# A Mamba/GLA trunk: decay broadcasts on ScalarE's queue, weight stores on SyncE's, block sums in three stages, PSUM banks shared out anew

## The chip, the cores and the metric

One core of one Trainium2 chip runs the whole kernel. The metric is the device time of one launch in microseconds (us). Before the change three runs gave 2479.24, 2486.99 and 2486.57 us, a median of 2486.57 us.

## What is computed

The reference is one layer of a hybrid decoder over 2048 tokens and 16 meta tokens, width 1024. One input projection feeds two branches, their results are gated and merged, and an output projection follows.

```python
u = rmsnorm(hres, norm_w)
proj = jnp.einsum('bld,dn->bln', u, w_in)
z, xbc, dt_raw, q, k, v, g_gla, a_lr, merge_g = split_cols(proj, IN_WIDTHS)
xbc = jax.nn.silu(causal_depthwise_conv(xbc, conv_w, conv_b))
dt = jax.nn.softplus((dt_raw + dt_bias).astype(jnp.float32))
y_r, _ = ssd_chunked(xs[:, m:], dt[:, m:], a, bm[:, m:], cm[:, m:], SSD_CHUNK, s_m)
y_ssd = rmsnorm((y.reshape(b, l, D_SSD) * jax.nn.silu(z)).reshape(...), ...)   # 4 groups of 4 heads
o_r, _ = gla_chunked(q[:, m:], k[:, m:], v[:, m:], log_a[:, m:], GLA_CHUNK, st_m)   # 4 heads
y_gla = o.reshape(b, l, GLA_DV) * jax.nn.silu(g_gla)
branch_proj = jnp.einsum('blnc,ncd->blnd', branches, w_branch)
merged = jnp.sum(gates * branch_proj, axis=2)
return hres + jnp.einsum('bld,de->ble', merged, w_out)      # then a final rmsnorm
```

Within an SSD chunk the scores are multiplied by `exp(da_cum[t] - da_cum[s])`, so each chunk needs the cumulative decay of its four heads broadcast to all 128 partitions.

## The kernel before

**Two phases.** The first runs to 1667 us of the profile. It takes the tokens in four blocks of 512 and does the projections and the scans of both branches. The second does the gate, branch and output matmuls by a scheme of seven products in place of eight, for which sums of quarter blocks (`sums`) are needed as moving operands.

**The first phase, per block.** Four SSD groups (`ssd_proj`, `ssd_scan`) and then four GLA heads (`gla_proj`, `gla_scan`). The projection generators run in the foreground. At each of their `yield`s the main loop calls `step()`, which advances every background generator by one step: the scan of the group before, the `gates`, the load of the next block's `u`, and a unit of block sums (`beside_unit`). A group or head has 6 steps. TensorE (PE) and SyncE (SP) execute in exactly this written order (`manual_schedule`); the orders of ScalarE (ACT), VectorE (DVE) and GpSimd (POOL) come from a scheduler.

**Matmuls.** Each product in high precision is three matmuls (`accum`, L174 to L176: high by high, high by low, low by high). `proj_feat` makes 128 features by all tokens of the block: 24 matmuls of 512 columns per half weight, or, in block 0, where the 16 meta tokens come first, two segments of 264 columns in two PSUM banks. `proj_tok` makes tokens by 256 features for z (SSD) and v (GLA): four chunks of 128 tokens, each in a PSUM bank of its own, although it fills half of one.

**Weights.** In block 0 `load_w` loads each weight tile to `wr` (3 buffers, L160), ACT copies the high part to `whl` (4 buffers, L161), POOL subtracts to get the low part (L162), and the pair is stored to DRAM from ACT's queue (`save`, L170). There are 100 such tiles. Blocks 1 to 3 load the kept pair in one DMA (L157, names `k_s`, `k_z`, `k_g`, `k_v`, `k_zm`). A load waits until PE has done with the tile four before it.

**Decay broadcasts.** `dt_chain` transposes the cumulative decay, ACT copies it to `th` (L385) and stores it to the DRAM tile `cumd` (L386). `fetch_cb` loads one chunk's rows back, broadcast over partitions, to `cb` (2 buffers, L468, 64 DMAs on SP). The first of a group is issued after that group's third feature projection, the next ones in `before(c)` of the scan. ACT reads `cb` in the Relu at L527.

**Block sums.** `make_sums` loads four 128x256 pieces to two `wr` tiles on SP (L76), subtracts on POOL (L80) in the same step, and stores four results from ACT's queue (L84) one step later. Six units of eight such pieces run in the first phase, one (`late`) in the second.

**PSUM.** Eight banks: four `pj` (projections and gates), two `pt` (transposes), two `pc` (scan matmuls). At the end of an SSD scan two transposes into `pt` are read by ACT (L575); at the end of a GLA scan two are read by DVE (L779). The next transposes on PE are those of another scan: L483 and L515 (SSD), L686 and L691 (GLA). Feature projections are read from `pj` by ACT at L447 and L448 (SSD) and L588 (k of GLA), and the gates at L411.

Of the kernel before, what the change touches and what calls it, by code (L numbers as in the profile page):

```python
# [14 lines left out]
P = 128  # L15
# [25 lines left out]
def trunk_kernel(ctx: ExitStack, tc: tile.TileContext, xm, xmt, w_feat, w_tok, w_zm, w_br, w_o,  # L41
# [24 lines left out]

    HB = BLK // 2
# [3 lines left out]
    def make_sums(pool, tag, nb, braw, sums, j, c, store):  # L71
        cs = slice(c * HB, (c + 1) * HB)
        room = [mk(pool, [P, 512], F32, tag, bufs=nb) for _ in range(2)]
        room = [t[:, i * HB:(i + 1) * HB] for t in room for i in range(2)]
        for r, (k, t) in zip(room, ((0, 1), (0, 0), (1, 1), (1, 0))):
            nc.sync.dma_start(r, braw(4 * k + j, t)[:, cs])  # L76
        b12, b11, b22, b21 = room
        todo = []
        for i, (o, x, y) in enumerate(((b11, b12, b11), (b12, b22, b12), (b22, b22, b11), (b21, b21, b22))):
            nc.gpsimd.tensor_tensor(o, x, y, op=ALU.subtract)  # L80
            todo.append((sums[(0, 2, 1, 3)[i]][j][:, cs], o))
        yield
        for dst, src in todo:
            store.dma_start(dst, src)  # L84

    def new_sums(name):
        return [[left(f"{name}_t{i}_{j}") for j in range(4)] for i in range(4)]
# [31 lines left out]
    pj = first.enter_context(tc.tile_pool(name="pj", bufs=4, space=bass.MemoryType.PSUM))  # L119
    pt = first.enter_context(tc.tile_pool(name="pt", bufs=2, space=bass.MemoryType.PSUM))  # L120
# [32 lines left out]
    def load_w(key, src):  # L153
# [4 lines left out]
        else:  # L158
            raw = mk(wpool, [P, 512], F32, "wr", bufs=NWR)[:, :n]
# [7 lines left out]
    def save(n):  # L167

        while len(unsaved) > n:
            nc.scalar.dma_start(*unsaved.pop(0))  # L170
# [19 lines left out]
    def proj_tok(key, src, u, starts, pools, width=256, per=2, sub=None):  # L190


        pss = [bank(*pl) for pl in pools]
        nq = KT // per
        for q0 in range(0, nq, 2):
# [3 lines left out]
            for i, (ps, a) in enumerate(zip(pss, starts)):  # L199
                c0 = sub if sub is not None and i >= NCH else 0  # L200
                for k2 in range(2 * per):
# [4 lines left out]
                          (h[:, cs], lo[:, cs]), kt == 0, kt == KT - 1)  # L206
        return pss
# [131 lines left out]
    def dt_chain(o, psd):  # L339
# [44 lines left out]
        cr = mk(wk, [P, META + BLK], F32, "th", bufs=1)[:NH, :BLK]  # L384
# [39 lines left out]
    def ssd_proj(o, g):  # L424
# [3 lines left out]
        if g == 0:  # L428
            pools = [(pj, "pj")] * NCH + ([(pc, "pc")] if m0 else [])
            pss = yield from proj_tok("zm", w_zm, o.u, o.starts + [0] * o.ci0, pools, 288, 1, 256)  # L430
            begin(dt_chain(o, pss[NCH:] + pss[:NCH]))
            pss = pss[:NCH]
        else:
            pss = yield from proj_tok(f"z{g}", w_tok[g], o.u, o.starts, [(pj, "pj")] * NCH)
        for c, ps in enumerate(pss):
            zt = mk(wk, [P, 256], F32, "zt", bufs=1)
            nc.scalar.activation(zt, ps[:, :256], AF.Tanh, scale=0.5)
            nc.vector.scalar_tensor_tensor(zs[:, c], zt, 1.0, ps[:, :256], op0=ALU.add, op1=ALU.mult)
        yield
        for j in range(4):  # L440
# [13 lines left out]
            th = mk(wk, [P, META + BLK], F32, "th", bufs=1)[:, :tt]  # L454
            nc.scalar.activation(th, acc, AF.Tanh)
            f = mk(wk, [P, META + BLK], F32, "act", bufs=NACT)
            nc.vector.scalar_tensor_tensor(f[:, :tt], th, 1.0, acc, op0=ALU.add, op1=ALU.mult)
            feats.append(f)
            if j == 2:
                fetch_cb(o, g, 0)  # L460
# [5 lines left out]
    def fetch_cb(o, g, c):  # L466
        cbs[g, c] = cb = mk(wk, [P, 4, P], F32, "cb")
# [654 lines left out]
```

## Time and profile before

| | |
|---|---|
| median of three runs | 2486.57 us |
| the profiled execution, its own time | 2480.0 us |
| its span, first to last instruction | 2478.2 us |
| first phase, blocks 0, 1, 2, 3 (from the start) | 0 to 455, to 848, to 1242, to 1667 us |
| second phase | 1667 to 2478 us |
| PE busy | 2295.6 us (93%) |
| DVE, ACT, POOL busy | 1584.5, 1192.5, 736.9 us |
| mean granted clock of TensorE | 0.964 |

A row of waits reads "who, at which line and tile, waited for whom: us in total, times, longest us". A row of a timeline reads "start us, us, engine, line, operation, tiles, count" and in brackets the idle time just before, with what ended it. Rows that begin with SPq or ACTq are of an engine's queue, which issues DMAs and waits in order. Rows of windows give the stretch, its length, the busy time of PE, weight loads, DVE, ACT and POOL, the granted clock, the share of the DMA engines, and GB/s. A matmul's own duration overlaps the next one's: what matters is the distance of starts.

### The profile page before, as it was taken

How to read it: one execution, taken by the hardware profiler on the slowest of the kernel's cores; microseconds unless marked ns; L12 is line 12 of the kernel's file. 1: busy time of each engine (PE TensorE's matmuls, PEld its weight loads, DVE VectorE, ACT ScalarE, POOL GpSimd, SP SyncE). 2: the span in 40 equal slices, each digit the busy share in tenths (PEclk: the TensorE clock that was granted, in tenths of full speed). 3: DMA queues.
4: the chain of work that ended last, by engine and by line, in shares of the span. 5: the costliest groups of instructions: out<-in, count | busy, mean ns of one | idle time of the engine just before them, and what ended most of it. 6: DMA issues, size and time to landing. Idle time of an engine off the chain costs nothing. (4 is left out here: it accounts for less than half of the span.)

```text
span 2478.2 us, 37092 instructions
## 1 busy us (share of the span) xinstructions
PE 2295.6 (93%) x12641; PEld 1989.2 (80%) x12641; DVE 1584.5 (64%) x2913; ACT 1192.5 (48%) x2820; POOL 736.9 (30%) x713
## 2 busy tenths in 40 slices
PE   6899999979989989999989999979999999999898
PEld 6789889868878977888877888858888778888676
DVE  3577665656566557655546565576478874788865
ACT  4565555445543346444335543445455444553443
POOL 2334433122320122231022112245433642335431
PEclk8899999989999999999999999979999999999999
DMA  7555765466785556686465567657477853777653
GB/s 252 201 181 212 269 242 188 158 218 216 232 273 179 178 173 223 222 264 207 156 203 190 180 196 233 203 171 258 146 263 247 270 197 108 259 236 261 211 158 127
DMA packets 303342, 518.10 MB, mean 209 GB/s; under 512 B 29488, under 2 KB 145456, under 8 KB 303152
## 3 DMA queue, kind: packets, MB, share of 16 engines
q1 hardware_dynamic: 246128, 414.65, 52.3%
q10 hardware_dynamic: 57024, 101.08, 10.9%
q8 instruction: 99, 1.62, 0.3%
q14 instruction: 91, 0.75, 0.1%
HBM read 368.42 MB, written 147.19 MB: 208 GB/s over the span
## 5 line engine op out<-in xcount | busy, mean ns | idle before, releaser
L174 PE MATMUL pj<-u,whl 128*128 128x512 f32 (+1 forms) x1184 | 454.1, 384 | 50.4 <-DMA whl<-k_s 31.7
L176 PE MATMUL pj<-u,whl 128*128 128x512 f32 (+1 forms) x1184 | 437.5, 370 | 1.5 <-POOL whl L162 1.5
L175 PE MATMUL pj<-u,whl 128*128 128x512 f32 (+1 forms) x1184 | 437.0, 369 | 0.0
L174 PE MATMUL pj<-whl,u 128*128 128x256 f32 (+1 forms) x1024 | 303.8, 297 | 14.7 <-ACT u L273 6.5
L174 PEld LDWEIGHTS pj<-u,whl 128*128 128x128 f32 x1184 | 231.0, 195 | 92.4 <-DMA whl<-k_s 35.3
L175 PE MATMUL pj<-whl,u 128*128 128x256 f32 (+1 forms) x1024 | 297.3, 290 | 1.6 <-POOL whl L162 1.5
L176 PE MATMUL pj<-whl,u 128*128 128x256 f32 (+1 forms) x1024 | 296.9, 290 | 1.4 <-DVE u L275 1.4
L176 PEld LDWEIGHTS pj<-u,whl 128*128 128x128 f32 x1184 | 229.5, 194 | 38.8 <-POOL whl L162 2.1
L175 PEld LDWEIGHTS pj<-u,whl 128*128 128x128 f32 x1184 | 230.8, 195 | 34.1
L174 PE MATMUL psa<-b,a 128*128 128x512 f32 x640 | 249.0, 393 | 3.4 <-ACT b L870 1.9
L175 PE MATMUL psa<-b,a 128*128 128x512 f32 x640 | 250.6, 392 | 0.1
L176 PE MATMUL psa<-b,a 128*128 128x512 f32 x640 | 247.3, 391 | 0.4 <-DVE a L892 0.4
L174 PEld LDWEIGHTS pj<-whl,u 128*128 128x128 f32 x1024 | 201.3, 197 | 17.2 <-DMA whl<-k_v 7.1
L452 DVE SCALAR_TENSOR_TENSOR acc<-cin,hcw,acc 128x512 f32<-128x512 f32 (+1 forms) x192 | 154.3, 803 | 80.3 <-ACT acc L448 79.5
L175 PEld LDWEIGHTS pj<-whl,u 128*128 128x128 f32 x1024 | 201.2, 196 | 3.0 <-POOL whl L162 2.7
L176 PEld LDWEIGHTS pj<-whl,u 128*128 128x128 f32 x1024 | 201.1, 196 | 1.9 <-DVE u L275 1.8
L162 POOL TENSOR_TENSOR whl<-wr,whl 128x512 fp32r<-128x512 f32 (+1 forms) x100 | 132.4, 1333 | 200.6 <-ACT whl L161 131.8
L871 DVE TENSOR_TENSOR b<-br,b 128x512 fp32r<-128x512 f32 x196 | 168.0, 898 | 25.1 <-ACT b L870 25.1
L80 POOL TENSOR_TENSOR wr<-wr 128x256 f32<-128x256 f32 x96 | 74.8, 779 | 318.2 <-DMA wr<-y 161.7
L882 POOL TENSOR_TENSOR as<-ar,ar 128x512 f32<-128x512 f32 x40 | 59.8, 1496 | 328.5 <-DMA ar<-in_w_br 106.0
L892 DVE TENSOR_TENSOR a<-ar,a 128x512 fp32r<-128x512 f32 x160 | 140.6, 891 | 20.7 <-ACT a L891 20.6
L174 PEld LDWEIGHTS psa<-b,a 128*128 128x128 f32 x640 | 121.3, 190 | 30.4 <-ACT sn L908 2.7
(259 smaller groups left out, 5100.5 us busy)
## 6 DMA issues: line engine op xcount, KB each, us to landing
whl<-k_s SPq DMA_DIRECT2D x96, 512.0 KB, 5.3
whl<-k_g SPq DMA_DIRECT2D x96, 512.0 KB, 4.2
whl<-k_v SPq DMA_DIRECT2D x48, 512.0 KB, 4.2
whl<-k_z SPq DMA_DIRECT2D x36, 512.0 KB, 4.1
wr<-in_w_feat SPq DMA_DIRECT2D x64, 256.0 KB, 4.4
k_s<-whl ACTq DMA_DIRECT2D x32, 512.0 KB, 4.3
cb<-cumd SPq DMA_DIRECT2D x64, 256.0 KB, 5.2
y<-gg ACTq DMA_DIRECT2D x64, 256.0 KB, 3.0
```

Source lines behind the costliest of these rows:

```text
L80: nc.gpsimd.tensor_tensor(o, x, y, op=ALU.subtract)
L162: nc.gpsimd.tensor_tensor(hl[:, 1], raw, hl[:, 0].bitcast(F32), op=ALU.subtract)
L174: nc.tensor.matmul(ps, sh, mh, start=first, stop=False, **kw)
L175: nc.tensor.matmul(ps, sh, ml, start=False, stop=False, **kw)
L176: nc.tensor.matmul(ps, sl, mh, start=False, stop=last, **kw)
L452: nc.vector.scalar_tensor_tensor(acc, cin[:, k:k + tt], hcw[:, ti, k:k + 1], acc, op0=ALU.mult, op1=ALU.add)
L871: nc.vector.tensor_tensor(t[:, 1], raw, t[:, 0].bitcast(F32), op=ALU.subtract)
L882: nc.gpsimd.tensor_tensor(s1, a21, a22, op=ALU.add)
L892: nc.vector.tensor_tensor(t[:, 1], src, t[:, 0].bitcast(F32), op=ALU.subtract)
```

## The change

1. `fetch_cb` issues on ACT's queue, `cb` has 3 buffers, and the first fetch of a group moves from the projection to the start of its scan.
2. The kept weights of block 0 are stored from SP: `load_w` calls `save(2)` just ahead of each new load.
3. `make_sums` has a step for the loads, one for the subtractions and one for the stores; two results that lie side by side are stored in one DMA. A unit takes 24 steps where it took 16. The units are placed at group 0 and group 4, five in the first phase, two in the second.
4. Two chunks of z (groups 1 to 3) and of v share a bank; they are read in operations of 512 columns. `pj` has 3 banks, `pt` has 3. The fourth chunk of the first z lies in a `pt` bank.
5. The tiles `th` and `zt` are gone: tanh is written to its destination and multiplied in place. The copy for `cumd` uses a `cin` buffer.

```diff
     def make_sums(pool, tag, nb, braw, sums, j, c, store):
         cs = slice(c * HB, (c + 1) * HB)
-        room = [mk(pool, [P, 512], F32, tag, bufs=nb) for _ in range(2)]
-        room = [t[:, i * HB:(i + 1) * HB] for t in room for i in range(2)]
-        for r, (k, t) in zip(room, ((0, 1), (0, 0), (1, 1), (1, 0))):
+        pair = [mk(pool, [P, 512], F32, tag, bufs=nb).rearrange("p (i c) -> p i c", i=2) for _ in range(2)]
+        for r, (k, t) in zip((t[:, i] for t in pair for i in range(2)), ((0, 1), (0, 0), (1, 1), (1, 0))):
             nc.sync.dma_start(r, braw(4 * k + j, t)[:, cs])
...
+        yield
+        (b12, b11), (b22, b21) = [(t[:, 0], t[:, 1]) for t in pair]
+        for o, x, y in ((b11, b12, b11), (b12, b22, b12), (b22, b22, b11), (b21, b21, b22)):
             nc.gpsimd.tensor_tensor(o, x, y, op=ALU.subtract)
         yield
-        for dst, src in todo:
-            store.dma_start(dst, src)
+        for dst, src in zip(sums, pair):
+            store.dma_start(dst[j][:, :, cs], src)
...
-    beside = {(1, 0): ("o",)}
+    beside = {(1, 0): ("o",), (1, 4): ("g", 0)}
+    late = []
     for s in range(nsb):
-        b = 2 * s + 1
-        if b + 1 < nblk:
-            beside.update({(b, 3): ("g", s), (b + 1, 0): ("b", 0, s), (b + 1, 3): ("b", 1, s)})
+        b = 2 * s + 2
+        if b < nblk:
+            beside.update({(b, 0): ("b", 0, s), (b, 4): ("b", 1, s)})
         else:
-            beside.update({(b, 0): ("g", s), (b, 5): ("b", 0, s)})
-    late = [("b", 1, nsb - 1)]
+            late += [("b", 0, s), ("b", 1, s)]
+        if 0 < s:
+            beside[b - 1, 0] = ("g", s)
...
-    pj = first.enter_context(tc.tile_pool(name="pj", bufs=4, space=bass.MemoryType.PSUM))
-    pt = first.enter_context(tc.tile_pool(name="pt", bufs=2, space=bass.MemoryType.PSUM))
+    pj = first.enter_context(tc.tile_pool(name="pj", bufs=3, space=bass.MemoryType.PSUM))
+    pt = first.enter_context(tc.tile_pool(name="pt", bufs=3, space=bass.MemoryType.PSUM))
...
         else:
+            save(2)
             raw = mk(wpool, [P, 512], F32, "wr", bufs=NWR)[:, :n]
             nc.sync.dma_start(raw, src)
...
         while len(unsaved) > n:
-            nc.scalar.dma_start(*unsaved.pop(0))
+            nc.sync.dma_start(*unsaved.pop(0))
...
                     accum(ps[:, c0:width], tuple(t[:, kt, a:a + P] for t in u),
-                          (h[:, cs], lo[:, cs]), kt == 0, kt == KT - 1)
-        return pss
+                          (h[:, cs], lo[:, cs]), bk not in opened, kt == KT - 1, skip_group_check=True)
+                    opened.add(bk)
+
+    def halves_of(pool, tag):
+
+        bks = [bank(pool, tag) for _ in range(2)]
+        return bks, [(i // 2, bks[i // 2][:, i % 2 * 256:(i % 2 + 1) * 256]) for i in range(4)]
...
-        cr = mk(wk, [P, META + BLK], F32, "th", bufs=1)[:NH, :BLK]
+        cr = mk(wk, [P, 3 + META + BLK], F32, "cin")[:NH, :BLK]
...
-        for c, ps in enumerate(pss):
-            zt = mk(wk, [P, 256], F32, "zt", bufs=1)
-            nc.scalar.activation(zt, ps[:, :256], AF.Tanh, scale=0.5)
-            nc.vector.scalar_tensor_tensor(zs[:, c], zt, 1.0, ps[:, :256], op0=ALU.add, op1=ALU.mult)
+            pss, places = halves_of(pj, "pj")
+            yield from proj_tok(f"z{g}", w_tok[g], o.u, o.starts, places)
+            done = [(ps, zs[:, 2 * r:2 * r + 2].rearrange("p c f -> p (c f)")) for r, ps in enumerate(pss)]
+        for ps, dst in done:
+            nc.scalar.activation(dst, ps, AF.Tanh, scale=0.5)
+            nc.vector.scalar_tensor_tensor(dst, dst, 1.0, ps, op0=ALU.add, op1=ALU.mult)
...
             feats.append(f)
-            if j == 2:
-                fetch_cb(o, g, 0)
             yield
...
-        cbs[g, c] = cb = mk(wk, [P, 4, P], F32, "cb")
-        nc.sync.dma_start(cb, o.cumd[4 * g:4 * g + 4, c * P:(c + 1) * P].unsqueeze(0).to_broadcast([P, 4, P]))
+        cbs[g, c] = cb = mk(wk, [P, 4, P], F32, "cb", bufs=3)
+        nc.scalar.dma_start(cb, o.cumd[4 * g:4 * g + 4, c * P:(c + 1) * P].unsqueeze(0).to_broadcast([P, 4, P]))
 
     def ssd_scan(o, g, feats, zs):
...
         x0, x1, bf, cf = feats
+        fetch_cb(o, g, 0)
         yield
```

On SP the decay fetch leaves the stream of weight loads. Before, block 1, from the second feature of group 0 to the first z weight of group 1 (`whl` weight tiles, `cb` a decay broadcast, `wr` pieces of the block sums):

```order
L157 DMA whl_5689<-k_s_0_757 128x1024
L157 DMA whl_5703<-k_s_1_787 128x1024
L157 DMA whl_5789<-k_s_0_844 128x1024
L157 DMA whl_5803<-k_s_1_874 128x1024
L468 DMA cb_5830<-cumd_5318 128x4x128
L76 DMA wr_5852<-in_w_o 128x256 x2
L76 DMA wr_5853<-in_w_o 128x256 x2
L157 DMA whl_5863<-k_s_0_925 128x1024
L157 DMA whl_5877<-k_s_1_955 128x1024
L157 DMA whl_5918<-k_z_0_1007 128x1024
```

After, the same place:

```order
L159 DMA whl_5534<-k_s_0_696 128x1024
L159 DMA whl_5548<-k_s_1_727 128x1024
L76 DMA wr_5620<-in_w_o 128x256 x2
L76 DMA wr_5621<-in_w_o 128x256 x2
L159 DMA whl_5635<-k_s_0_782 128x1024
L159 DMA whl_5649<-k_s_1_813 128x1024
L159 DMA whl_5700<-k_s_0_860 128x1024
L159 DMA whl_5714<-k_s_1_891 128x1024
L159 DMA whl_5750<-k_z_0_939 128x1024
```

The weights of the fourth feature (`k_s_0_925`, now `k_s_0_860`) and of z no longer stand behind `cb`, and the pieces of the block sums stand one projection earlier here.

On ACT, block 0, group 0, the fetches now stand right behind the store of `cumd`. Before (`pj` are projection banks, `th` the copy that is stored):

```order
L385 ACTIVATE th_832<-pt_827 16x512
L447 ACTIVATE cin_899<-pj_837 128x264
L448 ACTIVATE acc_900<-pj_837,hcb,hcw 128x264
L447 ACTIVATE cin_899<-pj_838 128x264
L448 ACTIVATE acc_900<-pj_838,hcb,hcw 128x264
L386 DMA cumd_442<-th_832 16x512
L161 ACTIVATE whl_920<-wr_921 128x512
```

After:

```order
L394 ACTIVATE cin_771<-pt_766 16x512
L395 DMA cumd_386<-cin_771 16x512
L164 ACTIVATE whl_933<-wr_935 128x512
L455 ACTIVATE cin_838<-tails 128x3
L475 DMA cb_995<-cumd_386 128x4x128
L465 ACTIVATE act_763<-acc_753 128x528
L455 ACTIVATE cin_916<-tails 128x3
L475 DMA cb_1094<-cumd_386 128x4x128
L475 DMA cb_1214<-cumd_386 128x4x128
L457 ACTIVATE cin_838<-pj_774 128x264
L458 ACTIVATE acc_839<-pj_774,hcb,hcw 128x264
```

Three fetches are issued together, ahead of the third feature's evacuation. The order on PE is the same in both kernels.

More of the change, by code (lines that the diff above doesn't have):

```diff
@@ L188, in proj_feat, with proj_tok @@
         return pss
-    def proj_tok(key, src, u, starts, pools, width=256, per=2, sub=None):
-        pss = [bank(*pl) for pl in pools]
+    def proj_tok(key, src, u, starts, banks, width=256, per=2, sub=None):
         nq = KT // per
+        opened = set()
         for q0 in range(0, nq, 2):
@@ L592, in gla_proj @@
         vm = None
+        pss, places = halves_of(pj, "pj")
         if m0:
             vm = mk(wk, [P, 256], F32, "c1", bufs=NC1)[:META]
[L595 to L601 removed]
+            pv5 = bank(pt, "pt")
+            places.append((2, pv5[:, :256]))
+        yield from proj_tok(f"v{h}", w_tok[SG + h], o.u, o.starts + [0] * o.ci0, places)
+        if m0:
+            nc.scalar.activation(vm, pv5[:META, :256], AF.Copy)
+        for r, ps in enumerate(pss):
+            split(*[t[:, 2 * r:2 * r + 2].rearrange("p c f -> p (c f)") for t in (vh, vl)], ps)
         yield
@@ L814, in trunk_kernel @@
                     step()
-                    save(2)
             save(0)
@@ L1027, in trunk_kernel @@
                 gen = make_sums(rpl, "tb", 2, *sums[key], j, c, nc.sync)
-                for _ in range(2):
-                    at(i, lambda gen=gen: next(gen, None))
-                    i += 3
+                for k in range(3):
+                    at(i + 2 * k, lambda gen=gen: next(gen, None))
+                i += 5
     for fn in todo.get(-1, []):
```

37 lines of the change are left out of this document (12 added, 25 removed).

## The prediction

> **What bounds the kernel now.** I read the page first, then the waits of PE, then of SP, then timelines around the longest waits, and the granted clock in windows last.
>
> ```profile
> span 2478.2 us, 37092 instructions
> PE 2295.6 (93%) x12641; PEld 1989.2 (80%) x12641; DVE 1584.5 (64%) x2913; ACT 1192.5 (48%) x2820; POOL 736.9 (30%) x713
> ```
>
> PE is the bound, and the other engines have room on average. The change takes no matmul away and leaves PE's order as it was, so all it can win is PE's idle time, 2478.2 - 2295.6 = 183 us, and time in which PE runs at a lower clock. The next view names what PE waited for.
>
> ```profile
> PE pj L174 <- DMA whl<-k_s: 31.7, 8, 8.7
> PE pt L515 <- DVE gg L779: 14.0, 3, 5.3
> PE pj L174 <- ACT whl L161: 12.6, 3, 7.3
> PE pt L691 <- ACT gg L575: 12.1, 4, 5.4
> PE pj L174 <- DMA whl<-k_v: 5.3, 4, 2.1
> PE pt L483 <- ACT gg L575: 5.0, 3, 2.5
> PE pj L174 <- DMA whl<-k_g: 4.5, 2, 2.3
> PE pt L686 <- ACT gg L575: 1.9, 1, 1.9
> ```
>
> There are two families. One waits for weights, though in blocks 1 to 3 these come ready from DRAM. The other (L483, L515, L686, L691) are transposes that wait for a `pt` bank until the last two transposes of the scan before are read. The long waits of the first family, in order of time:
>
> ```profile
> 74.92 0.59 PE L174 MATMUL pj<-u,whl 128*128 128x264 f32 x1 [7.34 <-ACT whl L161]
> 503.68 0.80 PE L174 MATMUL pj<-u,whl 128*128 128x512 f32 x1 [8.68 <-DMA whl<-k_s]
> 896.96 0.80 PE L174 MATMUL pj<-u,whl 128*128 128x512 f32 x1 [7.95 <-DMA whl<-k_s]
> 1289.96 0.79 PE L174 MATMUL pj<-u,whl 128*128 128x512 f32 x1 [8.13 <-DMA whl<-k_s]
> ```
>
> One per block, at the same place: the fourth feature of group 0. SP's own waits, then its timeline, then one row of ACT's say why.
>
> ```profile
> SPq L160 <- POOL whl L162: 215.6, 74, 9.1
> SPq L468 <- ACT sq L527: 138.8, 23, 18.9
> SPq L468 <- DMA cumd<-th: 73.8, 4, 20.8
> ...
> 471.04 3.04 SPq L157 DMA_DIRECT2D whl<-k_s  x2
> 494.91 0.37 SPq L468 DMA_DIRECT2D cb<-cumd  x1
> 495.38 1.88 SPq L76 DMA_DIRECT2D wr<-in_w_o  x4
> 497.35 0.86 SPq L157 DMA_DIRECT2D whl<-k_s  x2
> ...
> 493.32 0.32 ACTq L386 DMA_DIRECT2D cumd<-th  x1
> ```
>
> SP issued weights until 474.08, then stood for 20.8 us in front of the decay fetch, because ACT stored `cumd` only at 493.32; it had landed when the fetch went out at 494.91. The weights behind it in SP's order were issued at 497.35, and PE stood until 503.68. The four such waits (73.8 us on SP) answer to the four on PE.
>
> **The clock.** After such a wait PE also runs slower for a while.
>
> ```profile
> 503.70:508.70 5.00, 5.00 (x12) 3.94 (x13) 0.00 (x0) 0.00 (x0) 0.00 (x0) 0.50 0.89 320
> 549.60:553.00 3.40, 3.39 (x14) 3.21 (x15) 3.40 (x8) 0.24 (x2) 0.00 (x0) 0.52 0.27 101
> 943.70:949.00 5.30, 5.29 (x18) 4.74 (x19) 5.30 (x13) 0.69 (x3) 0.65 (x1) 0.50 0.28 103
> 1336.90:1341.60 4.70, 4.68 (x17) 4.22 (x18) 4.70 (x12) 0.41 (x2) 0.65 (x1) 0.50 0.30 112
> 745.00:835.00 90.00, 89.22 (x553) 79.98 (x553) 52.16 (x129) 38.30 (x107) 4.39 (x2) 1.00 0.53 169
> ```
>
> Behind the 8.68 us wait the granted clock is 0.50 for 5 us, so 2.5 us more are lost. Behind the three waits at L515 (549.61, 943.7, 1336.9) it is 0.50 to 0.52 for 3.4, 5.3 and 4.7 us, a loss of 1.6 + 2.65 + 2.35 = 6.6 us. The last row is the counterexample: 90 us of GLA heads of block 1 with no block sums and no decay fetch, where PE is busy 89.22 us at clock 1.00. The other engines can keep up when nothing blocks. The Trainium skill states this as a rule ("TensorE: Matmul & The Clock Gate", Part 1): about one window of 3.4 us idle drops the clock to half, about one of busy work restores it. The rows agree on the half; by the page alone a long wait would cost an estimated 1.7 us more, by the rows 1.6 to 2.65.
>
> **The change, part by part.** The sum is made against the profiled execution's 2480.0 us, which is 6.6 us under the median of 2486.57; the forecast is put on the median.
>
> *Decay fetch to ACT.* The four waits go: 7.34 + 8.68 + 7.95 + 8.13 = 32.1 us. The clock behind them, taken at 2.2 us each (between 1.6 and 2.65), is 9 us. What is late next: on ACT the fetch now waits for the landing of `cumd`, 494.9 - 493.3 = 1.6 us, four times, with the evacuation of a projection queued behind it on ACT. Its wait for a free `cb` cannot pass to ACT, since ACT's own Relu is what frees it. The fetch stands many instructions ahead of its Relu, where the fetch took 5.2 us (row below). I take 41 - 3 = 38 us; bounds 20 (other waits step in for half) and 41.
>
> ```profile
> cb<-cumd SPq DMA_DIRECT2D x64, 256.0 KB, 5.2
> k_s<-whl ACTq DMA_DIRECT2D x32, 512.0 KB, 4.3
> ```
>
> The Trainium skill speaks against this part ("DMA: Bandwidth & Descriptors", Issuing engines are not separate DMA queues): starting DMAs on several engines saves only the time to issue them. By that alone this part would bring next to nothing; it has a rival below.
>
> *Other weight waits.* Of 31.7 us for `k_s`, 8.68 + 7.95 + 8.13 = 24.8 are counted; 6.9 remain, with 5.3 (`k_v`) and 4.5 (`k_g`), 16.7 in all. SP stood 138.8 us in front of `cb` for a free buffer, which goes; the loads of the next block's rows and of the sums remain in SP's order. I take half, 8 us; bounds 0 and 17.
>
> *Three transpose banks.* The pattern is two transposes, then one more that needs the first bank. A third bank lets it start at once; the one after that comes a projection later. At L515 and L691 14.0 + 12.1 = 26.1 us go, plus 6.6 us of clock at L515. In block 0 the meta tokens need two banks in a row (L483, then L515), so of 5.0 + 1.9 us a third goes, 2 us. That is 35 us. The reads by DVE and ACT are no sooner done, so some of it comes back when PE needs their later results: I take 28; bounds 14 and 35.
>
> *Three projection banks.* In blocks 1 to 3 a projection takes one bank and has the time of two others to be read. In block 0 it takes two of three, and the next one's second segment needs the first one's bank:
>
> ```profile
> 55.11 0.56 ACT L448 ACTIVATE acc<-pj,hcb,hcw 128x264 f32<-128x264 f32 x1
> ...
> 55.29 0.37 PE L174 MATMUL pj<-u,whl 128*128 128x264 f32 x1
> ...
> 225.55 0.47 PE L174 MATMUL pj<-u,whl 128*128 128x264 f32 x1
> ...
> 227.31 0.56 ACT L448 ACTIVATE acc<-pj,hcb,hcw 128x264 f32<-128x264 f32 x1
> ```
>
> The second segment begins after three matmuls; at 443 matmuls of 512 columns in 100 us (row at 1690, below) one takes 0.226 us, and three of 264 columns 0.35. In the best case the bank is read at 55.67 and wanted at 55.64, a wait of nothing; in the worst it is read at 227.87 and wanted at 225.90, 2.0 us. 12 projections of block 0 follow another closely (three in each SSD group), and the gates once: 13 places. Bounds 0 and 26; nearer the low end, since ACT reads within a microsecond of the matmuls where no scan runs. I take 10 us lost.
>
> *Stores of kept weights on SP.* SP waits there for POOL's low part. The next load waits for that too (215.6 us, row above), so the store adds no wait in front of it. A load may stand behind a 512 KB store in the same queue; 4.3 us for a store is the nearest row. PE waited for ACT's weight copy only 12.6 us in three places, one of them counted above. I take 0; bounds 0 and -8. If weights were short in block 0, this is where the cover would be gone.
>
> *Block sums.* The extra unit of the second phase adds 32 subtractions of about 0.79 us and their DMAs on POOL and SP, where PE had next to no idle:
>
> ```profile
> 1690.00:1790.00 100.00, 100.00 (x443) 82.81 (x442) 52.47 (x62) 45.35 (x82) 49.54 (x38) 1.00 0.56 181
> 1790.00:1920.00 130.00, 128.77 (x566) 105.56 (x565) 104.39 (x135) 71.36 (x130) 45.02 (x28) 1.00 0.75 249
> L80 POOL TENSOR_TENSOR wr<-wr 128x256 f32<-128x256 f32 x96 | 74.8, 779 | 318.2 <-DMA wr<-y 161.7
> ```
>
> The first of these stretches already holds the one unit and PE is busy throughout; POOL has half of its time free. I take 1 us lost; bounds +3 and -8. In the first phase POOL no longer stands in front of the landing of pieces; PE was not waiting for that, so nothing.
>
> *Wider reads and tanh in place.* Fewer instructions on DVE and ACT, beside PE. They free `pj` of z sooner. Nothing; the cover is the projection in the third bank.
>
> *New lateness.* With some 70 us of waits gone, ACT and DVE have less time to catch up. The row at 745 says it can go without loss, but block sums and SSD scans were not in it. I take 12 us lost; bounds 0 and 25.
>
> Sum: 38 + 8 + 28 - 10 - 1 - 12 = 51 us. 2480.0 - 51 = 2429 for the profiled execution, **2436 us** on the median.
>
> **The rivals.** *All waits go.* 41 + 17 + 35 with 5 lost at the banks: 88 us, 2399. For it speaks the stretch at 745; against it that every stall gave the other engines time.
>
> *The waits come back elsewhere.* Half of the decay part (20) and half of the banks (14), less 10 and 4: 20 us, 2467. For it: DVE's reads at L779 were late by themselves, and PE follows with work that needs DVE.
>
> *The queue does not matter.* The DMA engines are the limit, and a fetch from ACT is worth no more than one from SP. Then the decay part is 0 and the sum 51 - 38 = 13 us, 2473. Against it stands the timeline: from 474.08 to 494.91 SP issued nothing, so no DMA engine could have been the limit. This is the page's rule on issuing engines; the wait in the queue ahead of the issue is outside its words.
>
> *ACT becomes the blocked queue.* All of L468's waits, 138.8 + 73.8 = 212.6 us, move to ACT, ahead of evacuations, and with three banks PE has one projection (24 matmuls at 0.226 us, 5.4 us) of slack instead of two. If a third of that reaches PE, 71 us, the sum is 20 us slower, 2507. It decides where ACT stands for over 5 us between two evacuations. Against it: 138.8 us of the wait are for ACT itself, which does not wait for itself, and 1.6 us per block remain of the rest.
>
> *The change does not do what it says*: the written order shows the fetch off SP, so I give it no chance of its own.
>
> **How the numbers follow.** The forecast 0.63, all waits go 0.12, back elsewhere 0.12, the queue does not matter 0.05, ACT blocked 0.08. A measurement of this kernel can tell 0.3%, 7.5 us. Faster takes all but the last and the low end of the two before it: 0.87; same 0.06; slower 0.07. The range reaches from 2385, the case in which all waits go with a little more of the clock behind them, to 2474, the case of the queue. Outside lie the blocked ACT and the ends of the others, about 0.15.
>
> **What would show it.** Right: SP's wait for `cumd` gone, no wait over 5 us of PE for `whl<-k_s`; the four L174 rows without their brackets; L515 and L691 below 5 us together; the clock over blocks 1 to 3 nearer 1.00; new waits of PE for ACT at L457 and L458 below 15 us in block 0. Wrong: long waits of ACT for `cb` or `cumd` in front of evacuations, weights of block 0 late behind stores, or waits on DVE in the sum of what has gone.

## The result, and the profile after

| | before | after |
|---|---|---|
| median (lowest to highest), 4 runs each, same chip | 2486.78 us (2479.24 to 2490.01) | 2407.7 us (2399.34 to 2411.83) |
| ratio, 95% interval | | 0.9682 [0.9648, 0.9716] |
| profiled execution: own time, span | 2480.0, 2478.2 us | 2399.34, 2397.5 us |
| granted clock of that execution | 0.964 | 0.975 |

The change is 79 us faster. That lies in the range, and 28 us beyond the 51 us that were forecast. First the page of the changed kernel.

```profile
span 2397.5 us, 36613 instructions
PE 2271.9 (95%) x12641; PEld 1972.0 (82%) x12641; DVE 1575.3 (66%) x2857; ACT 1182.7 (49%) x2764; POOL 736.5 (31%) x713
```

The same 12641 matmuls now keep PE busy for 2271.9 us instead of 2295.6 (23.7 less), and PE's idle time fell from 183 to 2397.5 - 2271.9 = 126 us (57 less). So some 30% of the gain is not idle time at all; it goes with the clock. An estimate from the two mean clocks says the same: (1 - 0.964) of 2478.2 us is 89 us, (1 - 0.975) of 2397.5 us is 60.

The next two views give the busy time by stage: blocks 0 to 3 of the first phase, each counted from its first projection matmul, then the second phase. Columns: the stretch and its length; busy time and count of PE, PEld, DVE, ACT and POOL; granted clock; DMA share; GB/s. Before:

```profile
15.00:449.50 434.50, 396.17 (x2681) 367.51 (x2682) 271.58 (x521) 236.41 (x604) 156.28 (x142) 0.94 0.62 216
449.50:847.10 397.60, 367.05 (x2165) 323.57 (x2164) 237.25 (x532) 185.01 (x486) 78.76 (x108) 0.97 0.64 207
847.10:1239.90 392.80, 363.83 (x2163) 321.32 (x2162) 236.69 (x531) 184.73 (x485) 78.61 (x108) 0.97 0.65 210
1239.90:1667.00 427.10, 388.02 (x2269) 339.81 (x2267) 252.70 (x564) 192.94 (x514) 98.66 (x127) 0.95 0.62 196
1667.00:2478.20 811.20, 777.84 (x3360) 634.74 (x3360) 581.62 (x749) 383.66 (x716) 321.64 (x220) 0.98 0.64 211
```

After:

```profile
15.40:432.90 417.50, 387.85 (x2683) 361.57 (x2683) 263.71 (x507) 233.54 (x590) 154.72 (x142) 0.96 0.66 225
432.90:797.90 365.00, 356.77 (x2166) 316.56 (x2164) 238.82 (x518) 182.04 (x471) 78.50 (x108) 1.00 0.69 226
797.90:1162.80 364.90, 357.10 (x2163) 316.82 (x2161) 235.20 (x517) 181.85 (x471) 77.53 (x108) 0.99 0.70 226
1162.80:1560.90 398.10, 380.21 (x2269) 335.18 (x2267) 248.84 (x551) 191.77 (x500) 78.02 (x96) 0.97 0.58 190
1560.90:2397.50 836.60, 787.16 (x3360) 639.51 (x3360) 583.96 (x749) 383.68 (x716) 344.79 (x250) 0.97 0.64 214
```

Each of blocks 0 to 3 is 17 to 33 us shorter, 106 us in all. In block 1 PE is idle for 8.2 of 365.0 us at clock 1.00, where it was idle for 30.6 of 397.6 at 0.97. The second phase goes the other way: 836.6 against 811.2 us, 25 us back, with PE busy 9.3 us longer at a lower clock and POOL busy 23.2 us longer. The net, 106 - 25, is the 81 us of the two spans.

The longest waits of PE after the change (us in total, times, longest):

```profile
PE psb L179 <- DVE a L899: 16.9, 9, 5.0
PE pc L745 <- DVE c L688: 13.0, 15, 4.1
PE psa L177 <- ACT a L898: 11.0, 1, 11.0
...
PE pj L417 <- ACT g_all L420: 4.6, 2, 3.8
PE pt L523 <- ACT gg L583: 2.9, 1, 2.9
...
PE pt L699 <- ACT gg L583: 2.1, 1, 2.1
...
PE pj L177 <- DMA whl<-k_g: 2.0, 2, 1.3
...
PE pj L177 <- ACT acc L458: 0.8, 3, 0.3
```

No wait for `whl<-k_s` is left among PE's waits, and the transposes of L515 and L691, now L523 and L699, wait 5.0 us instead of 26.1. The third row is new, one wait of 11.0 us; it belongs to the second phase. In block 1, the place that the prediction showed at 503.68, SP and ACT now read so:

```profile
454.83 10.81 SPq L159 DMA_DIRECT2D whl<-k_s  x4
470.30 3.04 SPq L159 DMA_DIRECT2D whl<-k_z  x2
473.43 2.42 SPq L76 DMA_DIRECT2D wr<-in_w_o  x4
```

```profile
468.25 0.33 ACTq L395 DMA_DIRECT2D cumd<-cin  x1
470.44 0.20 ACT L455 ACTIVATE cin<-tails 128x3 f32<-128x3 f32 x1 [2.22 <-DMA cumd<-cin]
470.45 0.94 ACTq L475 DMA_DIRECT2D cb<-cumd  x2
```

The 20.8 us hole in SP's stream is gone. ACT waits 2.22 us for `cumd` to land, about what the prediction charged. But look at when `cumd` is stored: 35.4 us after the block's first matmul at 432.9, where it was 43.8 us before (493.32 - 449.50). The fetch does not make the store earlier: with the fetch alone moved (a run below) `cumd` is still stored 43.7 us into block 1. One other thing that changed is the buffer: the copy that is stored lies in a `cin` buffer now; before, it went into the one `th` buffer, in which ACT also put the tanh of every feature.

### The profile page after: what moved, and what is told of

Same layout as the page of the kernel before. It is cut to its first block, busy times and chain, and to the rows that moved or that the text cites. A ratio compares the mean times of both kernels' runs of the same rounds, so it can differ in the third digit from the quotient of the medians.

```text
span 2397.5 us, 36613 instructions
## 1 busy us (share of the span) xinstructions
PE 2271.9 (95%) x12641; PEld 1972.0 (82%) x12641; DVE 1575.3 (66%) x2857; ACT 1182.7 (49%) x2764; POOL 736.5 (31%) x713
## 5 line engine op out<-in xcount | busy, mean ns | idle before, releaser
L177 PE MATMUL pj<-u,whl 128*128 128x512 f32 (+1 forms) x1184 | 448.9, 379 | 7.6 <-ACT whl L164 2.5
L179 PE MATMUL pj<-u,whl 128*128 128x512 f32 (+1 forms) x1184 | 433.1, 366 | 0.8 <-POOL whl L165 0.8
L178 PE MATMUL pj<-u,whl 128*128 128x512 f32 (+1 forms) x1184 | 432.4, 365 | 0.0
L177 PE MATMUL pj<-whl,u 128*128 128x256 f32 (+1 forms) x992 | 290.9, 293 | 9.5 <-ACT u L282 6.3
L179 PE MATMUL pj<-whl,u 128*128 128x256 f32 (+1 forms) x992 | 284.6, 287 | 1.3 <-DVE u L284 1.3
L178 PE MATMUL pj<-whl,u 128*128 128x256 f32 (+1 forms) x992 | 284.6, 287 | 0.6 <-POOL whl L165 0.5
L177 PEld LDWEIGHTS pj<-u,whl 128*128 128x128 f32 x1184 | 226.9, 192 | 45.3 <-ACT whl L164 2.9
L179 PEld LDWEIGHTS pj<-u,whl 128*128 128x128 f32 x1184 | 226.6, 191 | 37.1 <-POOL whl L165 1.1
L178 PEld LDWEIGHTS pj<-u,whl 128*128 128x128 f32 x1184 | 227.3, 192 | 33.6
L177 PEld LDWEIGHTS pj<-whl,u 128*128 128x128 f32 x992 | 191.7, 193 | 11.2 <-ACT u L282 6.7
L80 POOL TENSOR_TENSOR wr<-wr 128x256 f32<-128x256 f32 x80 | 65.0, 812 | 438.6 <-DMA wr<-y 178.2
L878 DVE TENSOR_TENSOR b<-br,b 128x512 fp32r<-128x512 f32 x196 | 176.0, 938 | 31.5 <-ACT b L877 31.4
L179 PEld LDWEIGHTS pj<-whl,u 128*128 128x128 f32 x992 | 191.9, 193 | 2.0 <-DVE u L284 2.0
L178 PEld LDWEIGHTS pj<-whl,u 128*128 128x128 f32 x992 | 191.8, 193 | 1.8 <-POOL whl L165 1.3
```

What stands on the lines that cost most here:

```text
L177: nc.tensor.matmul(ps, sh, mh, start=first, stop=False, **kw)
L178: nc.tensor.matmul(ps, sh, ml, start=False, stop=False, **kw)
L179: nc.tensor.matmul(ps, sl, mh, start=False, stop=last, **kw)
L878: nc.vector.tensor_tensor(t[:, 1], raw, t[:, 0].bitcast(F32), op=ALU.subtract)
```

## The experiments

Where several kernels are compared, a difference in us is the difference of their ratios times 2480; each ratio is against runs of the kernel before on the same chip. The intervals make such a difference good to some 5 to 12 us. Blocks and phases are read from one profiled execution of each kernel. Two kernels below have exactly the first phase of the changed one: their block 0 took 414.9 and 421.2 us and their first phase 1550.7 and 1548.8, against 417.5 and 1545.5. Differences of that size say nothing.

### The decay fetch: queue or place

Two edits of the changed kernel. One puts the fetch back where it was, on SP behind the third feature and with two buffers:

```diff
             feats.append(f)
+            if j == 2:
+                fetch_cb(o, g, 0)
...
-        cbs[g, c] = cb = mk(wk, [P, 4, P], F32, "cb", bufs=3)
-        nc.scalar.dma_start(cb, o.cumd[...])
+        cbs[g, c] = cb = mk(wk, [P, 4, P], F32, "cb")
+        nc.sync.dma_start(cb, o.cumd[...])
...
-        fetch_cb(o, g, 0)
```

> The changed kernel with the decay fetch alone put back: on SP, after the third feature projection, two buffers. Theory (the fetch blocked SP in front of weights, and this was the largest part): the four waits of 7 to 9 us at the fourth feature of group 0 come back with the slower clock behind them, about 41 us, plus some short waits for whl in the SSD groups: 2445 to 2465 us, SP's wait for cumd near 70 us. Rival (the queue does not matter, the DMA engines are the limit): 2400 to 2415 us.

The other keeps the new place and the three buffers and changes the queue alone: `nc.scalar.dma_start(cb, ...)` becomes `nc.sync.dma_start(cb, ...)`.

> The changed kernel with the fetch on SP but at its new, later place and with three buffers. If the queue is what matters (SP still waits there for cumd or for a free buffer ahead of weights): SP's waits at the fetch come back to some 60 us or more and the time is 2420 to 2450 us. If the place and the third buffer are what matters: SP's waits at the fetch stay under 30 us and the time is within 6 us of the changed kernel's 2408.

And the fetch alone in the kernel before: on ACT at the scan's start, with the two buffers of before.

```diff
             feats.append(f)
-            if j == 2:
-                fetch_cb(o, g, 0)
...
-        nc.sync.dma_start(cb, o.cumd[...])
+        nc.scalar.dma_start(cb, o.cumd[...])
...
+        fetch_cb(o, g, 0)
```

> The kernel before with the decay fetch alone moved: to ACT's queue and to the start of the scan, still two buffers. Theory (the fetch ahead of the weights in SP's order made the four long waits and, by its buffers, the short ones): PE's waits for whl<-k_s fall from 31.7 to under 5 us and the time is 30 to 45 us under the kernel before. Rival (cumd itself is late, so the wait only moves to ACT and from there to the projection banks): 0 to 15 us under it.

Measured: at the old place 2437.92 us, 0.9847 [0.9814, 0.9881], 41 us worse than the changed kernel. That is less than the 2445 to 2465 us expected. At the new place on SP 2404.82 us, 0.971 [0.968, 0.974], which cannot be told from the changed kernel's 0.9682 [0.9648, 0.9716]. Alone 2437.25 us, 0.9835 [0.98, 0.9869], a gain of 41 us. SP's order at the old place, block 1:

```profile
467.09 3.05 SPq L159 DMA_DIRECT2D whl<-k_s  x2
482.11 0.37 SPq L477 DMA_DIRECT2D cb<-cumd  x1
482.59 0.92 SPq L159 DMA_DIRECT2D whl<-k_s  x2
```

At the new place, also on SP:

```profile
473.51 3.04 SPq L159 DMA_DIRECT2D whl<-k_z  x2
476.60 1.85 SPq L76 DMA_DIRECT2D wr<-in_w_o  x4
478.54 0.38 SPq L475 DMA_DIRECT2D cb<-cumd  x1
```

At the old place SP issues nothing between 470.14 and 482.11, with weights of the fourth feature behind the fetch; at the new place the fetch goes out 0.1 us after the issue ahead of it. SP's waits in front of the fetch, summed, old place and then new:

```profile
SPq L477 <- ACT sq L536: 162.4, 17, 14.3
SPq L477 <- DMA cumd<-cin: 47.1, 4, 13.4
```

```profile
SPq L475 <- ACT sq L535: 37.8, 15, 6.7
SPq L475 <- DMA cumd<-cin: 3.6, 1, 3.6
```

The 41.4 us left at the new place lie between the 30 and the 60 us that the two theories had named; the time decides for the place. What is worth 41 us is that the fetch does not stand for long in front of the weight loads, and that is bought by the place in the order (on SP together with the third buffer, which no run here parts from it; on ACT's queue the fetch alone won as much with two). Which queue issues the fetch at its new place changed nothing measurable. That is what the Trainium skill says ("DMA: Bandwidth & Descriptors", Issuing engines are not separate DMA queues), and for the queue alone the trace agrees, 0.971 against 0.9682. The rule does not speak of a wait ahead of an issue, and it is in that wait that the two places differ. In the run of the fetch alone, SP's wait for `cumd` falls from 73.8 to 2.7 us and PE's for `whl<-k_s` is gone.

One more thing came out. With the fetch back at its old place, PE's wait for `whl<-k_s` stayed at 3.4 us in 3 waits, not 31.7 in 8 as before and as the theory had it; `cumd` is stored 35.4 us into block 1 here too, as in the changed kernel. The time was lost all the same, spread: block 0 is 12 us longer (429.4 against 417.5), blocks 1 to 3 are 3.6 to 8.6 us longer each, 30 us in the profiled executions, of which 20 are idle time of PE. So the four long waits were not the whole price of the place: most of it here is in many small waits that no single row names.

### Tanh in place

In the kernel before, only the scratch tile `th` goes: the tanh of a feature and of the gate is written into its own result, and the copy of `cumd` uses `cin`. The fetch stays on SP at its old place.

```diff
-        cr = mk(wk, [P, META + BLK], F32, "th", bufs=1)[:NH, :BLK]
+        cr = mk(wk, [P, 3 + META + BLK], F32, "cin")[:NH, :BLK]
...
-            nc.scalar.activation(th, acc, AF.Tanh)
-            nc.vector.scalar_tensor_tensor(f[:, :tt], th, 1.0, acc, op0=ALU.add, op1=ALU.mult)
+            nc.scalar.activation(f[:, :tt], acc, AF.Tanh)
+            nc.vector.scalar_tensor_tensor(f[:, :tt], f[:, :tt], 1.0, acc, op0=ALU.add, op1=ALU.mult)
```

> The kernel before with the single buffer th alone gone: tanh in place, the copy for cumd in a cin buffer; the fetch stays on SP at its old place. Theory (the single buffer made cumd late, and that is half of the long waits): cumd lands 5 to 8 us earlier after a block's start in blocks 1 to 3, the three waits of 8 us for whl<-k_s shrink to under 3 us each, and the time is 18 to 35 us under the kernel before. Rival (the place of the fetch is all of it): the waits stay over 5 us and the time is within 8 us of it.

Measured: 2458.8 us, 0.9916 [0.9886, 0.9946], a gain of 21 us from an edit that the prediction priced at nothing. One wait of PE, one of SP and the store of `cumd` in block 1, which begins at 443.2, in this kernel:

```profile
PE pj L174 <- DMA whl<-k_s: 15.7, 8, 3.8
```

```profile
SPq L467 <- DMA cumd<-cin: 57.8, 4, 17.2
```

```profile
483.46 0.32 ACTq L386 DMA_DIRECT2D cumd<-cin  x1
```

PE's waits for `k_s` fall from 31.7 to 15.7 us, the longest from 8.7 to 3.8, and SP's four waits for `cumd` from 73.8 to 57.8 us in all. The single buffer had delayed the store of `cumd`, and through SP's order the weights: 16 of the 21 us are that wait. But `cumd` is stored 40.3 us into the block, 3.5 us earlier than before and not the 5 to 8 expected, so the single buffer explains less than half of the way from 43.8 to 35.4. With the block sums alone changed (a run below) it is stored 41.2 us in. Every kernel here that has both edits stores it 34.9 to 35.4 us into block 1, whatever its banks, fetch and stores. This edit and the moved fetch attack the same stall, so their gains need not add; no run has these two alone.

### The banks

In the changed kernel, four projection banks and two for transposes again, one bank for each chunk of z and v:

```diff
-    pj = ...tile_pool(name="pj", bufs=3, ...)
-    pt = ...tile_pool(name="pt", bufs=3, ...)
+    pj = ...tile_pool(name="pj", bufs=4, ...)
+    pt = ...tile_pool(name="pt", bufs=2, ...)
...
-        bks = [bank(pool, tag) for _ in range(2)]
-        return bks, [(i // 2, bks[i // 2][:, i % 2 * 256:(i % 2 + 1) * 256]) for i in range(4)]
+        bks = [bank(pool, tag)[:, :256] for _ in range(4)]
+        return bks, list(enumerate(bks))
```

> The changed kernel with the old banks alone: four for projections, two for transposes, a bank for each chunk of z and v; tanh in place stays. Theory (the third transpose bank takes away PE's waits behind the last two transposes of a scan): the waits at L523 and L699 are 30 to 40 us together, the blocks 1 to 3 are 10 us longer each, block 0 some 5 to 10 us shorter: 2430 to 2445 us. Rival (those waits only came from PE being late or early by the weight waits): 2400 to 2415 us.

The banks alone in the kernel before, with z's tanh in place:

```diff
-    pj = ...tile_pool(name="pj", bufs=4, ...)
-    pt = ...tile_pool(name="pt", bufs=2, ...)
+    pj = ...tile_pool(name="pj", bufs=3, ...)
+    pt = ...tile_pool(name="pt", bufs=3, ...)
...
-            pss = yield from proj_tok(f"z{g}", w_tok[g], o.u, o.starts, [(pj, "pj")] * NCH)
+            pss, places = halves_of(pj, "pj")
+            yield from proj_tok(f"z{g}", w_tok[g], o.u, o.starts, places)
```

> The kernel before with the banks alone changed: three for projections, three for transposes, two chunks of z and v in one bank (z's tanh in place with it). Theory (the third transpose bank takes away PE's waits there, about as much as putting it back cost): PE's waits at the transposes fall from 33 to under 10 us, the four long waits for weights stay, and the time is 12 to 28 us under the kernel before. Rival (three projection banks cost in block 0 what the transposes gain): within 8 us of it, with block 0 over 8 us longer.

Measured: banks undone 2419.82 us, 0.9771 [0.9741, 0.98], 22 us worse. Banks alone 2467.32 us, 0.9954 [0.9935, 0.9972], 11 us better, just short of the 12 to 28 expected. Waits of PE for a transpose bank when they are undone:

```profile
PE pt L491 <- ACT gg L583: 6.7, 3, 4.2
PE pt L699 <- ACT gg L583: 6.3, 4, 2.9
PE pt L523 <- DVE gg L787: 6.0, 3, 2.3
```

19.0 us come back under these three names, against 5.0 for L523 and L699 with three banks: the mechanism is the one that the prediction gave, though less came back than the 30 to 40 us expected of this run. With the banks alone, PE's waits behind the last transposes of a scan fall from 33 us to under 5, as expected. Block 0, where three projection banks should have cost 10 us, takes 419.1 us with four and 417.5 with three, no more apart than two executions. In the kernel before with the banks alone a small part of that cost shows, PE's wait for the reads of projection banks:

```profile
PE pj L174 <- ACT acc L455: 4.6, 6, 1.5
```

### Kept weights on SP

In the changed kernel, the stores go back to ACT: `nc.sync.dma_start(*unsaved.pop(0))` becomes `nc.scalar.dma_start(*unsaved.pop(0))`.

> The changed kernel with the kept weights stored from ACT's queue, as before. Forecast's step: nothing either way, block 0 within 3 us of 417 and the time within 6 us of the changed kernel's. Rivals: stores in front of loads in SP's queue held up weights in block 0 (then it is 5 to 10 us faster here); or ACT's issuing and waiting for POOL held up evacuations (then it is 5 to 15 us slower here).

Measured: 2416.86 us, 0.9762 [0.9738, 0.9787], 20 us worse, from a step priced at nothing. Its block 0:

```profile
15.00:443.80 428.80, 395.52 (x2683) 367.47 (x2683) 268.97 (x507) 233.81 (x590) 154.83 (x142) 0.94 0.63 219
```

Against 417.50 us with PE busy 387.85 at 0.96, block 0 is 11.3 us longer, 3.6 of it idle time of PE and 7.7 PE busy longer at the lower clock. The second of these is uncertain: block 0 of the kernel with four buffers below, which has the stores on SP, shows PE busy for 393.1 us at 0.94 as well. The first phase as a whole is 17 to 22 us longer than in the three kernels whose first phase differs from this one by the stores alone. No single wait of PE accounts for that; the longest new one in block 0 is for DVE (`sq`, 5.7 us in 3). All kernels of this study that have the stores on SP and the fetch at its new place took 414.9 to 422.1 us for block 0; all that lack one of the two or both took 426.7 to 434.5. Blocks 1 to 3, where no kept weight is stored, are 2.5 to 5.3 us longer each. How a store on ACT's queue reaches PE was not settled.

### The block sums

The kernel before leaves one unit of sums to the second phase, the changed kernel two. Four edits of the changed kernel try what the 25 us of the second phase hang on. First, one of the two units goes back into the first phase:

```diff
-            late += [("b", 0, s), ("b", 1, s)]
+            late += [("b", 1, s)]
+            beside[b - 1, 5] = ("b", 0, s)
```

> The changed kernel with one of the two late units of block sums put back into the first phase (block 3, from the second GLA head on), so that the second phase holds one, as before the change. Theory (the second phase grew from 811 to 836 us because of the extra unit): the second phase is 811 to 817 us again, the first phase grows by 0 to 8 us, 2383 to 2398 us in all. Rival (the second phase lost by the three steps of the sums, or by entering it with less work prepared): it stays at 830 to 840 us and the total at 2403 to 2415.

Then both stay late, but POOL's own queue issues their stores: in `make_sums(rpl, "tb", 2, ..., nc.sync)` the last argument becomes `nc.gpsimd`.

> The changed kernel with the stores of the late block sums issued from POOL's queue, behind POOL's own subtraction, and no longer from SP's. Theory (in the second phase SP stands in front of these stores until POOL is done, with the loads of the next stage behind them): PE's wait of 11 us at the first change of stage goes, the second phase is 812 to 826 us, and the time is 2383 to 2398 us, on a base of 2478 for the kernel before. Rival (POOL's time, the ports or the DMA engines are what the extra unit costs): the wait stays and the second phase is 830 us or more.

Then the same with four buffers, `make_sums(rpl, "tb", 4, ..., nc.gpsimd)`.

> The changed kernel with the late sums stored from POOL's queue and four buffers tb in place of two, so that SP waits neither for POOL nor for a store to land before it loads the next piece. Theory (SP, standing in its order at the late sums with the next stage's operands behind them, makes the 11 us wait of PE at the first change of stage): SP's waits at tb fall from 83 us to under 25, the wait of PE falls under 4 us, the second phase is 812 to 820 us. Rival (the loads of the next stage are late for another reason: POOL and the DMA engines are simply busier): the wait stays over 8 us and the second phase is 824 us or more.

And four buffers and POOL's stores with only one unit late, both edits together:

> The changed kernel with one late unit back in the first phase, and the other one stored from POOL's queue with four buffers. If SP's waits at the late sums were all that was left of the loss: second phase 806 to 814 us and 2375 to 2383 us on a base of 2478 for the kernel before. If one late unit does not block SP at a change of stage anyway: the time is within 4 us of 2385.

| | median us | ratio, interval | second phase us |
|---|---|---|---|
| changed kernel | 2407.7 | 0.9682 [0.9648, 0.9716] | 836.6 |
| one unit back | 2385.3 | 0.9634 [0.9604, 0.9664] | 816.9 |
| stores from POOL | 2394.02 | 0.9656 [0.9628, 0.9684] | 826.6 |
| stores from POOL, 4 buffers | 2378.38 | 0.96 [0.9574, 0.9627] | 813.8 |
| the last, one unit back | 2385.0 | 0.9631 [0.9606, 0.9656] | 816.8 |

The chain in the changed kernel, at the first change of stage. SP's queue (`br_t<-tb` is the store of a sum, `br<-br_t` the operand of the next stage that reads it):

```profile
1716.52 0.53 SPq L83 DMA_DIRECT2D br_t<-tb  x1
...
1721.76 0.52 SPq L83 DMA_DIRECT2D br_t<-tb  x1
1722.38 1.52 SPq L871 DMA_DIRECT2D br<-br_t  x3
...
1724.46 0.38 SPq L871 DMA_DIRECT2D br<-br_t  x1
```

Then ACT and PE:

```profile
1729.95 0.63 ACT L877 ACTIVATE b<-br 128x512 fp32r<-128x512 f32 x1 [14.48 <-DMA br<-br_t]
1732.41 0.61 ACT L898 ACTIVATE a<-ar 128x512 fp32r<-128x512 f32 x1
```

```profile
1733.08 0.79 PE L177 MATMUL psa<-b,a 128*128 128x512 f32 x1 [10.97 <-ACT a L898]
```

The operands of the stage stand in SP's queue behind a store that waits for POOL, so ACT waits 14.48 us and PE 10.97. Over the whole kernel SP waits 52.0 us for POOL at these stores (before 29.5 in 19) and 31.2 us for a free `tb` buffer at the loads (before 9.7):

```profile
SPq L83 <- POOL tb L80: 52.0, 23, 6.9
SPq L76 <- DMA br_t<-tb: 31.2, 21, 3.0
```

With POOL issuing the stores, the waits of PE and SP read:

```profile
PE psa L177 <- ACT a L898: 10.6, 1, 10.6
```

```profile
SPq L76 <- DMA br_t<-tb: 82.8, 22, 7.5
```

The 52.0 us at L83 are gone, the 31.2 at L76 have become 82.8, and PE's wait stands, against the theory: SP now waits for the same slow chain one item later, at the load that needs the buffer. (The second phase is 10 us shorter even so; why stays open.) With four buffers:

```profile
1564.50:2378.30 813.80, 777.06 (x3360) 633.02 (x3360) 590.88 (x749) 383.89 (x716) 356.09 (x272) 0.99 0.66 220
```

```profile
SPq L76 <- DMA br_t<-tb: 38.7, 14, 7.7
```

The second phase is back at 813.8 us, clock 0.99, with both units still in it, and the wait of 10.6 us is gone from PE's list; SP's waits at `tb` fall to 38.7 us, not under the 25 expected. At 2378.38 us this is the fastest kernel of the study, 20 us under the changed one. Taking a unit out of the phase as well gains nothing more (the second phase is 3.0 us longer, and the first no shorter). So it was not the amount of POOL's work that cost 25 us, but the chain of load, subtraction and store, with SP standing in it up to the first change of stage. With four buffers the last subtraction starts 111 us into the phase, with two 160 us, just ahead of the stage that reads the sums; these runs do not part the sums being finished earlier from SP being free earlier. Four buffers with the stores left on SP were not tried.

The sums alone in the kernel before: three steps, paired stores, the new places, both units late.

```diff
-            store.dma_start(dst, src)
+            store.dma_start(dst[j][:, :, cs], src)
...
-    late = [("b", 1, nsb - 1)]
+            late += [("b", 0, s), ("b", 1, s)]
```

> The kernel before with the block sums alone changed (three steps, stores in pairs, the new places, two late units). Theory (the extra late unit costs 20 to 25 us in the second phase, and the first phase gains little from the sums): second phase 828 to 840 us, first phase within 8 us of before, 10 to 25 us slower than the kernel before. Rival (the three steps and one unit fewer in the first phase give back there what the second loses): within 8 us of it.

Measured: 2472.27 us, 0.9974 [0.9953, 0.9996]; a gain of 6 us. The profiled execution was the shortest of its ten (2461.47 to 2483.33 us); in it the first phase is 40 us shorter (1612 against 1652) and the second 21 longer, so by the ratio the first phase gains nearer 28. I had expected no such gain there. Two waits of PE in this kernel:

```profile
PE pj L175 <- DMA whl<-k_s: 18.1, 3, 6.2
```

```profile
PE psa L175 <- ACT a L892: 11.3, 1, 11.3
```

The wait for `k_s` falls from 31.7 us in 8, so the old sums, too, had a part in the late weights; through which buffer or engine stays open. The wait of 11 us in the second phase comes with the sums alone, then, and with one unit back in the first phase it is not among PE's waits.

Taken alone, in the profiled executions, the edits shorten the first phase by 44 us (fetch), 20 (tanh), 8 (banks) and 40 (sums), 112 together, without the stores on SP, which no run has alone; all of them together shorten it by 106. So the parts overlap, and each of these figures is good to several us at best.

## Why the prediction came out as it did

The direction and the mechanisms of the fetch and of the transpose banks were right; the sum was low by 28 us since three terms put at nothing were not nothing (the tanh in place, the stores on SP, the sums in the first phase), and the two that were to take away in the first phase took little. By phase: 52 us were forecast for the first and 106 came; 1 us of loss for the second and 25 came. These two errors have opposite signs. With 106 us won and only 1 lost the median would have been some 2382 us, below the range, so it is in part luck that the time lies in it. It lies nearer to the rival in which all waits go (2399) than to the forecast (2436).

- **Decay fetch, 38.** 41 both undone and alone. Alone, the mechanism is the one given: the waits for `k_s` are gone. Undone, 41 us have other parts, with only 3.4 us of waits for `k_s`, so that agreement is luck. The rival of the queue was wrong as a forecast of the time, 2473 against 2407.7. The step as titled, "to ACT", was half right: the four waits were SP's order, as the timeline said, but a new place on the same queue cures them as well. The prediction never asked what the same fetch would do later on SP.
- **Wider reads and tanh in place, 0.** 21 for the tanh of features and gates alone; the wider reads were only run together with the banks. This step failed plainly: it looked at the instructions on DVE and ACT and at `pj`, not at who else waits for the one `th` buffer. The trace of before held the question: the fetch was late because `cumd<-th` was stored only at 493.32, 43.8 us into the block, and the prediction did not ask why.
- **Other weight waits, 8.** Not measured by itself. PE's waits for `k_s`, `k_v` and `k_g` are nearly all gone (2.0 us in 2 for `k_g` is left among those listed), nearer the bound of 17.
- **Transpose banks 28, projection banks -10.** Net 18 forecast, 22 measured when undone, 11 alone. The -10 was too large: L458's reads made PE wait 0.8 us in three places in the changed kernel, and 4.6 us in six with the banks alone, where 13 places of up to 2.0 us had been allowed for.
- **Stores on SP, 0.** About 20 when undone, with 10 us of uncertainty either way. The bounds, 0 and -8, allowed no gain. What the stores did to ACT's queue was not priced; the argument was about SP alone.
- **Block sums, -1.** Two steps failed. For the first phase the prediction said that PE was not waiting for what the sums hold up, so nothing; alone they won some 28 to 40 us there, with PE's wait for `k_s` down by 13.6. The second phase lost 25, outside the bounds of +3 and -8. The stretch at 1690 that was taken for the price has POOL half idle and PE busy throughout, and that is right for POOL's time, though it holds only 16 of the late unit's 32 subtractions; what decided was SP's order behind POOL, at a stage change that this stretch does not hold.
- **New lateness, -12.** Not seen. Blocks 1 and 2 lose 8 us each to idleness at clock 0.99 to 1.00, and ACT's new wait for `cumd` is 6.8 us in 4.

The sizes undone one at a time, 41 + 22 + 20, are more than 79 already, with 20 of loss to set against them and the gains of the tanh and of the sums' first phase to add. They overlap: the fetch, the tanh and the sums each shorten the same wait for `k_s`. How the 106 us of the first phase divide among them exactly stays open.

## What to carry to other kernels

A queue that issues in order makes everything behind a waiting item late: before asking which engine should issue a transfer, look at what it waits for and put it behind loads that others need. When a transfer is late, follow it back through the buffer that its source was written to; a scratch tile with one buffer can hold up a consumer far away. When a wait is moved to another queue, look at where the same chain is waited for next: a new queue brought some 6 us here, within its interval, and more buffers beside it 14.

## What the runs showed of the hardware

The clock counts beside the stalls: 24 of the 81 us between the two profiled executions are the same matmuls done in less busy time, against 57 us of idle time. It also hides small causes, since it varies with no edit at all. Block 0 of the kernel with four buffers is the same as that of the changed kernel; PE was busy in it for 393.1 us at clock 0.94, against 387.9 at 0.96, although it was idle for less time, 28.1 us against 29.6. A few us of one block in one execution show nothing by themselves.
